# Attention beside two scans: TensorE's order written out in bursts, groups and scan parts

## The chip, the core and the metric

The kernel runs on one core of a Trainium2 chip. The metric is the device time of one execution in microseconds (us). TensorE (PE in the rows) multiplies matrices, VectorE (DVE), ScalarE (ACT) and GpSimd (POOL) work on elements, and SyncE (SP) issues most transfers.

## The reference

One layer of a hybrid encoder on 2048 tokens of width 1024: one input projection feeds attention with 8 heads (96 wide, values 64 wide, no mask) and an RWKV-7 mixer with 8 heads that is scanned forward and backward; both are gated and merged, and a mixture of 32 experts follows.

```python
h  = RMSNorm(x)
z  = h @ w_in
o1 = MLA(z_mla)        # softmax(q k^T / sqrt(96)) v, 8 heads, no mask
o2 = BiRWKV7(z_rwkv)   # forward and backward scans
m  = sigmoid(z_g1) * (o1 @ w_br_mla) + sigmoid(z_g2) * (o2 @ w_br_rwkv)
x  = x + m @ w_out
x  = x + HierMoE(RMSNorm(x))
```

## The kernel before

There are three phases. The first projects, normalizes and prepares operands. The second, `phase2`, holds attention and the scans, and is the one that changes. The third merges and runs the experts.

**Attention.** 8 heads times 4 blocks of 512 queries make 32 blocks. A block goes over 16 tiles of 128 keys. For each tile, `scores` forms a 128x512 bank of scores in three matmuls of split operands (L684 to L686), ScalarE takes the exponential into a tile `e` (L689), and VectorE (`accv`, odd tiles) or GpSimd (`acc`, even tiles) adds it up for the column sums. `av` multiplies four `e` tiles at a time with the values (L703). `finish` closes a block: column sums by matmuls (L713), the reciprocal (L716), four transposes (L719) and the product (L721). The exponential needs the row maxima beforehand, so `smax` (L664, one matmul, reduced by VectorE at L665) runs 24 tiles ahead of the scores, and `mrow` (L668 to L672) folds a block's maxima into its query operand. Scores, maxima, sums and transposes share a ring of four PSUM banks, `s`.

**The scans.** 32 steps, each for both directions (d = 0, 1). `operands` prepares a step ahead of time: two groups of products (L960, the "products" of a direction), masked by VectorE (L962), "inner" (L968) with its mask (L969), and two groups of transposes ("tokens", L975) of tiles that GpSimd scaled (L952), copied by ScalarE (L976). `step` is a chain: "state" (L1000, and its part of the output at L1013), copied out as `rs` by VectorE for d = 0 (L1008) and ScalarE for d = 1 (L1006); "solve" (L1021), copied to `mv` by VectorE and ScalarE (L1023, L1024); "update" (L1049), added into the next `mv` by VectorE (L1052); and "output" (L1031), copied by ScalarE (L1035). Each of these groups has two halves, one a direction, of 8 matmuls, and both halves lie in one bank, `rec` or `sa`. The multiplies at L1003 decay the state.

**What sets the order.** The program is written as generators, and `phase2` starts scan steps by a rule of pace, 32 steps over 29 blocks. The scheduler then orders the instructions of each engine by its own simulation. On TensorE it interleaves matmuls of attention and scans freely. Only the four matmuls of `av` stand in an order written by hand.

Of the kernel before, what the change touches and what calls it, by code (L numbers as in the profile page):

```python
# [21 lines left out]
NT = T // 128  # L22
# [580 lines left out]
def attention(k, aside):  # L603
# [5 lines left out]
    with ExitStack() as ctx:  # L609
# [15 lines left out]
        def raw_tile(h):  # L625

            return p.tile([128, 512], F32, name="raw" if h else "e", bufs=2 if h else 7)[0:96]
# [48 lines left out]
        def scores(B, u):  # L676
            khi, klo = KT[B.h]
            B.e[u] = []
            for i in range(2):
                kb = 2 * u + i  # L680
                b, c = kb // 4, slice(kb % 4 * 128, kb % 4 * 128 + 128)
                next(first)
# [4 lines left out]
                e = p.tile([128, 512], F32, name="e", bufs=7)  # L687
# [8 lines left out]
        def av(B, us):  # L696

            order = [(u, i) for u in reversed(us) for i in (1, 0)]
            seen = [False, False]
            with tc.high_priority(), tc.manual_schedule(engines={nc.tensor.engine}):  # L700
                for u, i in order:
                    r = slice(i * 64, i * 64 + 64)
                    nc.tensor.matmul(B.o[r], VT[B.h][:, 2 * u + i], B.e[u][i], start=(us[0] == 0 and not seen[i]),  # L703
                                     stop=(us[-1] == NT // 2 - 1 and u == us[0]))
                    seen[i] = True
            for u in us:
                B.e.pop(u)

        def finish(B):
# [5 lines left out]
            rd = p.tile([128, 8], F32, name="rd")  # L715
            nc.vector.reciprocal(rd, t[:, 0:8])  # L716
            t = k.ps2.tile([128, 512], F32, name="s", bufs=4)
            for i in range(4):
                nc.tensor.transpose(t[0:64, i * 128:(i + 1) * 128], rd[:, 2 * i:2 * i + 1].to_broadcast([128, 64]),  # L719
                                    k.ident)  # L720
# [7 lines left out]
        BL = []  # L728

        def ahead():  # L730

            for h, qs in blocks:
                if qs == 0:
                    load_head(h)
                BL.append(load_q(h, qs))
                if qs == 0:
                    load_v(h)
                if len(BL) == 1:
                    yield
                for j in range(16):  # L740
                    smax(BL[-1], j)
                    yield
                mrow(BL[-1])
            while True:
                yield

        first = ahead()
        next(first)
        yield
        for _ in range(16):  # L750
            next(first)
        yield
        for _ in range(8):
            next(first)
        for n in range(len(blocks)):
            yield
            for u in range(8):
                if u == 0:
                    B = BL[n]
                    B.o = k.ps2.tile([128, 512], F32, name="o", bufs=1)  # L760
                    B.acc = p.tile([128, 512], F32, name="acc")
                    B.accv = p.tile([128, 512], F32, name="accv", bufs=1)
                    B.e = {}
                scores(B, u)
                if u in (2, 4, 6):
                    av(B, (u - 2, u - 1))
                if u == 4 and n:
                    finish(BL[n - 1])
                if u in (2, 6) and n > 4:
                    next(aside, None)  # L770
            nc.vector.tensor_tensor(B.acc, B.acc, B.accv, op=OP.add)
            av(B, (6, 7))
            B.ob = p.tile([64, 512], F32, name="ob", bufs=1)
            nc.scalar.copy(B.ob, B.o[64:128])
            nc.vector.tensor_tensor(B.ob, B.o[0:64], B.ob, op=OP.add)
        finish(BL[-1])


class Rwkv:
# [135 lines left out]
    def load(self, j):  # L915
# [5 lines left out]
        bk = p.tile([128, 2, 2, 4, 2, 64], F32, name="bk", bufs=1)  # L921
        mv = p.tile([128, 2, 2, 2, 4, 64], F32, name="mv")
        ys = p.tile([128, 2, 2, 4, 64], F32, name="ys", bufs=1)
        self.pair[j] = st, bk, mv, ys
# [15 lines left out]
    def operands(self, n):  # L940
        k, p = self.k, self.p
        nc = k.nc
        if n % 2 == 0:
            self.load(n // 2)
        st, bk, _, _ = self.pair[n // 2]
        bs = p.tile([128, 2, 4, 128], F32, name="bks", bufs=1)
        ar = p.tile([128, 2, 4, 64], F32, name="arb")
        bt = p.tile([128, 2, 8, 64], F32, name="bkt")
        self.ops[n] = ar, bt
        for d in range(2):  # L950
            c, s = self.where(n, d)
            nc.gpsimd.tensor_tensor(bs[:, d], bk[:, s, d].rearrange("p g b t -> p g (b t)"),  # L952
                                    k.wc[:, d, :, c:c + 1].to_broadcast([128, 4, 128]), op=OP.mult)
        for d in range(2):
            c, s = self.where(n, d)
            m = self.mask[:, d:d + 1].to_broadcast([128, 4, 128])
            tv = self.bank("sa").rearrange("p (g t) -> p g t", t=128)
            for g in range(4):
                for e, r, ro in self.HEADS:
                    nc.tensor.matmul(tv[ro, g], bk[r, s, d, g, 1 - e], st[r, s, e, d, g], start=True, stop=True)  # L960
            for e, r, ro in self.HEADS:
                nc.vector.tensor_tensor(st[ro, s, e, d].rearrange("p g a t -> p g (a t)"), tv[ro], m[ro], op=OP.mult)  # L962
# [8 lines left out]
        for e, r, _ in self.HEADS:  # L971
            tv = self.bank("sa").rearrange("p (q t) -> p q t", t=64)
            for q in range(8):
                d, g = divmod(q, 4)
                nc.tensor.transpose(tv[:, q], bs[r, d, g], k.ident[r, r])  # L975
            nc.scalar.copy(bt[:, e], tv)  # L976

    def step(self, n):
        k, p = self.k, self.p
        nc, S = k.nc, k.scratch  # L980
        rd, i = divmod(n, 4)
        st, _, mv, ys = self.pair[n // 2]
        ar, bt = self.ops.pop(n)
        tt = self.tt[rd]
        Q = (slice(0, 4), slice(4, 8))
        bank = lambda name: self.bank(name).rearrange("p (q f) -> p q f", f=64)
# [5 lines left out]
        m0 = p.tile([128, 8, 64], F32, name="m0", bufs=1)  # L992
        t = bank("rec")
        y = bank("yy")
        rs = p.tile([128, 8, 64], F32, name="rs", bufs=1)
# [20 lines left out]
        t = bank("rec")  # L1016
        for d in range(2):
            c, s = self.where(n, d)
            for g in range(4):
                for e, r, _ in self.HEADS:  # L1020
                    nc.tensor.matmul(t[r, 4 * d + g], tt[r, d, g, i if d == 0 else 3 - i], rs[r, 4 * d + g],  # L1021
# [4 lines left out]
        def output():  # L1026
            for d in range(2):
                c, s = self.where(n, d)
                for g in range(4):
                    for e, r, _ in self.HEADS:  # L1030
                        nc.tensor.matmul(y[r, 4 * d + g], ar[r, d, g], mv[r, s, e, d, g], start=False,  # L1031
                                         stop=(d == 1 and g == 3))
            for d in range(2):
                c, s = self.where(n, d)
                nc.scalar.copy(ys[:, d, s], y[:, Q[d]])  # L1035
                if n % 2:
                    c0 = n - 1 if d == 0 else 31 - n
                    for e, r, _ in self.HEADS:
                        nc.sync.dma_start(S["y"][d, c0 * 64:c0 * 64 + 128, e * 256:e * 256 + 256]
                                          .rearrange("(c t) x -> t c x", t=64),  # L1040
                                          ys[r, d].rearrange("p s g f -> p s (g f)"))

        if n < 31:
            t = bank("rec")
            for d in range(2):
# [5 lines left out]
                for e, r, _ in self.HEADS:  # L1051
                    nc.vector.tensor_tensor(mn[r, sn, e, d], t[r, Q[d]], m0[r, Q[d]], op=OP.add)  # L1052
        output()


def rwkv(k, R):
    R.steps()
    R.operands(0)
    R.load_tt(0)
    yield  # L1060
    for n in range(32):
# [815 lines left out]
```

## Time and profile before

| | us |
|---|---|
| median of 3 runs | 3668.69 (3665.12 to 3672.79) |
| the profiled execution | 3667.47 |
| its span | 3665.7 |
| TensorE busy (matmul) in the span | 3390.9 (93%) |
| VectorE | 2570.1 (70%) |
| ScalarE | 1496.8 (41%) |
| GpSimd | 1395.7 (38%) |

The span runs from the first to the last instruction of the profiled execution. An engine's busy time is the time in which at least one of its instructions was running. The shares are means over three phases with different limits; the rows further down take the second phase by itself.

### The profile page before, as it was taken

Reading aid. Unit: us, or ns where it says so; the run is one execution under the profiler, and the core shown is the slowest. Engines: PE = TensorE matmul, PEld = TensorE weight load, DVE = VectorE, ACT = ScalarE, POOL = GpSimd, SP = SyncE. Lnnn points to the kernel's source line nnn. Section 1 sums busy time; section 2 is a strip of 40 time slices with the busy share of each in tenths; the row PEclk is TensorE's granted clock in tenths of the full one; section 3 lists DMA queues with packets and bytes.
Section 4 is the critical chain, followed back from the end, with each engine's and each line's share of the span. In section 5 each row is a group of like instructions: output and inputs, shape, how many; then the busy total and the mean of one; then the engine's idle time right before and its main releaser. Section 6 shows DMA issues by size and latency. Waiting matters only on the chain. (4 is left out here: it accounts for less than half of the span.)

```text
span 3665.7 us, 66865 instructions
## 1 busy us (share of the span) xinstructions
PE 3390.9 (93%) x25104; PEld 2448.3 (67%) x25104; DVE 2570.1 (70%) x4799; ACT 1496.8 (41%) x2834; POOL 1395.7 (38%) x1301
## 2 busy tenths in 40 slices
PE   8999999999988889999999999999689997999991
PEld 6778777777766656666666666655477886666660
DVE  6845677777887766676666666667766776678777
ACT  5322444445343333333333333334322222677772
POOL 1022322334222344444444444434423232665554
PEclk9999999999998889999999999999799998999995
DMA  5545767676554352233233332210545444788987
GB/s 177 170 150 171 218 197 208 197 200 202 202 179 144 114 135 77 72 106 97 74 110 96 94 92 66 56 36 12 164 144 150 135 131 169 283 319 322 336 328 301
DMA packets 392837, 589.71 MB, mean 161 GB/s; under 512 B 66880, under 2 KB 245184, under 8 KB 392512
## 3 DMA queue, kind: packets, MB, share of 16 engines
q1 hardware_dynamic: 380016, 546.36, 47.0%
q0 software_dynamic: 11920, 38.30, 2.8%
q8 instruction: 199, 3.26, 0.4%
q14 instruction: 126, 1.03, 0.1%
q10 hardware_dynamic: 576, 0.76, 0.1%
HBM read 380.78 MB, written 204.51 MB: 160 GB/s over the span
## 5 line engine op out<-in xcount | busy, mean ns | idle before, releaser
L689 ACT ACTIVATE e<-s 128x512 f32<-128x512 f32 x512 | 305.1, 597 | 547.3 <-PE s L686 534.8
L665 DVE TENSOR_REDUCE mx<-s 128x1 f32<-128x512 f32 x512 | 345.6, 684 | 240.2 <-PE s L664 236.6
L145 PE MATMUL z<-hhi,wlo 128*128 128x512 f32 (+1 forms) x1184 | 470.0, 397 | 2.4 <-POOL wlo L136 2.4
L144 PE MATMUL z<-hlo,whi 128*128 128x512 f32 (+1 forms) x1184 | 470.9, 398 | 0.2 <-DVE hlo L188 0.2
L694 POOL TENSOR_TENSOR acc<-acc,e 128x512 f32<-128x512 f32 x224 | 291.7, 1302 | 470.1 <-ACT e L689 460.5
L143 PE MATMUL z<-hhi,whi 128*128 128x512 f32 (+1 forms) x1184 | 469.2, 397 | 0.7 <-ACT hhi L187 0.3
L136 POOL TENSOR_TENSOR wlo<-wraw,whi 128x1024 fp32r<-128x1024 f32 x61 | 151.7, 2488 | 310.8 <-ACT whi L135 263.8
L145 PEld LDWEIGHTS z<-hhi,wlo 128*128 128x128 f32 (+1 forms) x1184 | 222.4, 188 | 62.4 <-issue 8.8
L144 PEld LDWEIGHTS z<-hlo,whi 128*128 128x128 f32 (+1 forms) x1184 | 222.5, 188 | 56.5 <-issue 3.9
L143 PEld LDWEIGHTS z<-hhi,whi 128*128 128x128 f32 (+1 forms) x1184 | 222.4, 188 | 55.0 <-issue 3.0
L703 PE MATMUL o<-e,v 128*64 128x512 f32 x1024 | 247.9, 602 | 4.5 <-ACT e L689 4.5
L694 DVE TENSOR_TENSOR accv<-accv,e 128x512 f32<-128x512 f32 x224 | 200.9, 897 | 71.8 <-ACT e L689 70.3
L498 ACT CAST wh<-wr 128x1024 fp32r<-128x1024 f32 x198 | 204.3, 1047 | 107.4 <-PE y L1578 54.0
L684 PE MATMUL s<-qhi,kh 128*128 128x512 f32 x512 | 236.7, 462 | 0.1
L499 POOL TENSOR_TENSOR wl<-wr,wh 128x1024 fp32r<-128x1024 f32 x70 | 186.8, 2690 | 124.8 <-ACT wh L498 124.7
L664 PE MATMUL s<-kh,qhi 128*128 128x512 f32 x512 | 227.5, 451 | 7.2 <-ACT qhi L498 6.8
L499 DVE TENSOR_TENSOR wl<-wr,wh 128x1024 fp32r<-128x1024 f32 x128 | 185.5, 1455 | 63.7 <-ACT wh L498 58.8
L685 PE MATMUL s<-qlo,kh 128*128 128x512 f32 x512 | 203.7, 398 | 0.0
L686 PE MATMUL s<-qhi,kl 128*128 128x512 f32 x512 | 203.1, 397 | 0.0
L684 PEld LDWEIGHTS s<-qhi,kh 128*128 128x128 f32 x512 | 96.4, 188 | 90.8 <-issue 68.6
L664 PEld LDWEIGHTS s<-kh,qhi 128*128 128x128 f32 x512 | 98.3, 193 | 55.2 <-issue 21.2
L703 PEld LDWEIGHTS o<-e,v 128*64 128x64 f32 x1024 | 66.6, 136 | 92.4 <-issue 80.0
(485 smaller groups left out, 8112.5 us busy)
## 6 DMA issues: line engine op xcount, KB each, us to landing
wr<-w_exp SPq DMA_DIRECT2D x198, 512.0 KB
wraw<-w_in SPq DMA_DIRECT2D x61, 512.0 KB
s_ye<-ye SPq DMA_DIRECT2D x33, 512.0 KB
s_ar<-ar SPq DMA_DIRECT2D x64, 256.0 KB
s_bk<-bk SPq DMA_DIRECT2D x64, 256.0 KB
s_zg<-zo SPq DMA_DIRECT2D x64, 256.0 KB
bk<-s_bk SPq DMA_DIRECT2D x32, 512.0 KB
stk<-s_ar SPq DMA_DIRECT2D x64, 256.0 KB
```

Source lines behind the costliest of these rows:

```text
L143: nc.tensor.matmul(t[:rows], hi[:, c, :rows], hhi[b][:, c], start=(c == 0), stop=False)
L144: nc.tensor.matmul(t[:rows], hi[:, c, :rows], hlo[b][:, c], start=False, stop=False)
L145: nc.tensor.matmul(t[:rows], lo[:, c, :rows], hhi[b][:, c], start=False, stop=(c == 7))
L498: k.nc.scalar.copy(hi, src)
L499: (eng or k.nc.vector).tensor_tensor(lo, src, hi.bitcast(F32), op=OP.subtract)
L664: nc.tensor.matmul(t, B.qhi[:, i * 128:(i + 1) * 128], KT[B.h][0][b], start=True, stop=True)
L665: nc.vector.tensor_reduce(B.mx[:, i, b:b + 1], t, axis=AX.X, op=OP.max)
L684: nc.tensor.matmul(t, khi[b][:, c], B.qhi, start=True, stop=False)
L685: nc.tensor.matmul(t, khi[b][:, c], B.qlo, start=False, stop=False)
L689: nc.scalar.activation(e, t, AF.Exp, scale=scale)
L694: eng.tensor_tensor(a, a, e, op=OP.add)
L703: nc.tensor.matmul(B.o[r], VT[B.h][:, 2 * u + i], B.e[u][i], start=(us[0] == 0 and not seen[i]), stop=(us[-1] == NT // 2 - 1 and u == us[0]))
```

## The change

TensorE's instructions of phase 2 are put under `manual_schedule`: they run as they are written, and the scheduler orders the other engines alone. The program is written anew for it.

A block is four quarters. A quarter is a burst of four times one maximum and one score (16 matmuls), then one part of a scan step, then the value products of the quarter before (4 matmuls), then another part. A step has seven parts: products of d = 0 and GpSimd's scaling; state; products of d = 1; solve and the first tokens; the other tokens; update and output; inner and the loads. Eight slots a block for seven parts give 8/7 step a block, so the scans end with block 28.

Beside that: the column sums stand a part ahead of the rest of `finish` (`sums`, `finish`), and the fold of `accv` into `acc` (`total`) and the output copies (`out`) follow a quarter later. `e` has 9 buffers (7 before), `accv` and `bk` two each (one before). The copy `rs` of d = 0 moves from VectorE to ScalarE. Loads of a scan pair are issued two pairs ahead. The first loads of attention are issued ahead of the scan's first operands. The counts of matmuls do not change.

```diff
-    def operands(self, n):
+    def products(self, n, d):
...
-            if d:
-                nc.scalar.copy(rs[:, Q[d]], t[:, Q[d]])
-            else:
-                nc.vector.tensor_copy(rs[:, Q[d]], t[:, Q[d]])
+            nc.scalar.copy(rs[:, Q[d]], t[:, Q[d]])
...
+        with tc.manual_schedule(engines={nc.tensor.engine}):
+            for n in range(len(blocks)):
+                B = BL[n]
+                B.acc = p.tile([128, 512], F32, name="acc")
+                B.accv = p.tile([128, 512], F32, name="accv")
+                B.e = {}
+                for v in range(4):
+                    scores(B, 2 * v)
+                    scores(B, 2 * v + 1)
+                    if v == 2 and n:
+                        sums(BL[n - 1])
+                    next(scan, None)
+                    if v:
+                        if v == 1:
+                            B.o = k.ps2.tile([128, 512], F32, name="o", bufs=1)
+                        av(B, (2 * v - 2, 2 * v - 1))
+                    elif n:
+                        av(BL[n - 1], (6, 7))
+                        out(BL[n - 1])
+                    next(scan, None)
+                    if v == 0 and n:
+                        total(BL[n - 1])
+                    if v == 2 and n:
+                        finish(BL[n - 1])
+                    if due:
+                        mrow(due.pop())
+                    if v % 2 and n > 4:
+                        next(aside, None)
...
+EB = 9
...
 def rwkv(k, R):
+
     R.steps()
-    R.operands(0)
+    R.load(0)
     R.load_tt(0)
+    for d in range(2):
+        R.products(0, d)
+    R.decayed(0)
+    for e in range(2):
+        R.tokens(0, e)
+    R.inner(0)
+    R.load(1)
     yield
     for n in range(32):
+        m = n + 1 if n < 31 else None
         if n % 4 == 0 and n < 28:
             R.load_tt(n // 4 + 1)
-        if n < 31:
-            R.operands(n + 1)
-        R.step(n)
+        if m:
+            R.products(m, 0)
+            R.decayed(m)
         yield
+        R.state(n)
+        yield
+        if m:
+            R.products(m, 1)
+        yield
+        R.solve(n)
+        if m:
+            R.tokens(m, 0)
+        yield
+        if m:
+            R.tokens(m, 1)
+        yield
+        R.update(n)
+        yield
+        if m:
+            R.inner(m)
+        if n % 2 and n // 2 + 2 < 16:
+            R.load(n // 2 + 2)
+        yield
+    R.ctx.close()
```

How the order moves is seen in three places in the middle of the stage. First TensorE around a solve, before; each row is a line, an operation, and what it writes and reads.

```order
L664 MATMUL s<-kh_12737,qhi_13324 128x512
L684 MATMUL s<-qhi_12773,kh_14127 128x512
L685 MATMUL s<-qlo_12774,kh_14127 128x512
L686 MATMUL s<-qhi_12773,kl_14129 128x512
L975 MATMUL sa<-cst,bks 128x64 x3
L703 MATMUL o<-e,v 64x512 x4
L664 MATMUL s<-kh_12746,qhi_13324 128x512
L1021 MATMUL rec<-rs,tt 64x64 x8
L684 MATMUL s<-qhi_12773,kh_14127 128x512
L685 MATMUL s<-qlo_12774,kh_14127 128x512
L686 MATMUL s<-qhi_12773,kl_14129 128x512
```

The eight matmuls at L1021 are one half of solve; score matmuls of attention stand on both sides, and the other half follows seven rows on. The same place of the changed kernel, with the semaphores that an instruction waits on; its lines are L716 for the sums, L968 for products, L701 for value products, L1053 for solve and L990 for tokens.

```order
L664 MATMUL s<-kh_13918,qhi_13080 128x512 [waits DVE_49]
L684 MATMUL s<-qhi_12679,kh_13909 128x512 [waits Activation_49]
L685 MATMUL s<-qlo_12680,kh_13909 128x512
L686 MATMUL s<-qhi_12679,kl_13911 128x512
L716 MATMUL s<-cst,acc 128x2 [waits DVE_49]
L716 MATMUL s<-cst,acc 128x2 x3
L968 MATMUL sa<-stk,bk 64x128 x8
L701 MATMUL o<-e,v 64x512 x4
L1053 MATMUL rec<-rs,tt 64x64 x8
L1053 MATMUL rec<-rs,tt 64x64 [waits Activation_49]
L1053 MATMUL rec<-rs,tt 64x64 x7
L990 MATMUL sa<-cst,bks 128x64 [waits PE_49,Pool_49]
```

The two halves of solve now stand back to back, and the first matmul of the second half waits on ScalarE. Next TensorE around an update, before.

```order
L1049 MATMUL rec<-mv,bkt 64x64 x3
L684 MATMUL s<-qhi_12773,kh_14127 128x512
L685 MATMUL s<-qlo_12774,kh_14127 128x512
L686 MATMUL s<-qhi_12773,kl_14129 128x512
L1049 MATMUL rec<-mv,bkt 64x64 x2
L664 MATMUL s<-kh_12737,qhi_13324 128x512
L1049 MATMUL rec<-mv,bkt 64x64 x3
```

One half of update stands in three pieces between score matmuls. The update of the changed kernel (L1069, output L1078), behind a group of value products:

```order
L990 MATMUL sa<-cst,bks 128x64 x8
L701 MATMUL o<-e,v 64x512 x4
L1069 MATMUL rec<-mv,bkt 64x64 x8
L1069 MATMUL rec<-mv,bkt 64x64 [waits DVE_49]
L1069 MATMUL rec<-mv,bkt 64x64 x7
L1078 MATMUL yy<-mv,arb 64x64 x16
```

Both halves and the output stand in one piece, the second half with a wait on VectorE. Last VectorE around an update, before.

```order
L721 TENSOR_TENSOR ob<-s,ob 64x512
L665 TENSOR_REDUCE mx<-s 128x1 x2
L1052 TENSOR_TENSOR mv<-rec,m_23721 64x256 x2
L665 TENSOR_REDUCE mx<-s 128x1
L694 TENSOR_TENSOR accv<-accv,e 128x512
L962 TENSOR_TENSOR stk<-sa,mask 64x512 x2
L665 TENSOR_REDUCE mx<-s 128x1
L1052 TENSOR_TENSOR mv<-rec,m_23721 64x256 x2
L1003 TENSOR_TENSOR m_24126<-mv,wc 64x256 x2
L665 TENSOR_REDUCE mx<-s 128x1
```

The two adds of a half (L1052) come with reductions of maxima between the halves. VectorE of the changed kernel, with L1072 for the adds, L710 for the fold of `accv`, L1034 for the decay and L1004 for inner's mask:

```order
L665 TENSOR_REDUCE mx<-s 128x1 x3
L694 TENSOR_TENSOR accv<-accv,e 128x512
L665 TENSOR_REDUCE mx<-s 128x1
L1072 TENSOR_TENSOR mv<-rec,m_18501 64x256
L694 TENSOR_TENSOR accv<-accv,e 128x512
L1072 TENSOR_TENSOR mv<-rec,m_18501 64x256
L710 TENSOR_TENSOR acc<-acc,accv 128x512
L1072 TENSOR_TENSOR mv<-rec,m_18501 64x256 x2
L1034 TENSOR_TENSOR m_18865<-mv,wc 64x256 x2
L1004 TENSOR_TENSOR arb<-sa,mask 128x256 x2
L665 TENSOR_REDUCE mx<-s 128x1 x3
```

A burst's reductions now come together, an add into `accv` stands between the two adds of update's first half, and the fold of `accv` ahead of those of the second.

## Rows read from the trace of the kernel before

**Rows 1.** Windows of all engines; after busy times the granted clock, DMA's share, GB/s.
```profile
1297.65:1420.00 122.35, 113.24 (x1226) 78.90 (x1226) 80.50 (x136) 40.81 (x76) 48.99 (x50) 0.93 0.46 120
1420.00:2400.00 980.00, 978.32 (x9008) 614.46 (x9003) 666.27 (x1096) 346.76 (x650) 437.13 (x417) 1.00 0.30 84
2400.00:2587.20 187.20, 174.67 (x925) 105.63 (x923) 125.98 (x187) 75.72 (x133) 84.35 (x68) 0.99 0.09 24
```
**Rows 2.** Timeline of TensorE around an update: start, duration, line, operation, count.
```profile
1701.97 0.50 PE L684 MATMUL s<-qhi,kh 128*128 128x512 f32 x1
...
1703.10 0.56 PE L1049 MATMUL rec<-mv,bkt 128*64 128x64 f32 x10
```
**Rows 3.** Timeline of TensorE in two late blocks, without scans.
```profile
2505.22 0.51 PE L684 MATMUL s<-qhi,kh 128*128 128x512 f32 x1
...
2509.10 1.94 PE L703 MATMUL o<-e,v 128*64 128x512 f32 x8
2510.97 0.51 PE L684 MATMUL s<-qhi,kh 128*128 128x512 f32 x1
...
2520.20 1.94 PE L703 MATMUL o<-e,v 128*64 128x512 f32 x8 [0.69 <-ACT e L689]
...
2524.36 0.95 PE L713 MATMUL s<-cst,acc 128*128 128x2 f32 x8
2526.51 1.02 PE L719 MATMUL s<-cst,rd 128*64 128x128 f32 x4 [1.21 <-DVE rd L716]
```
**Rows 4.** Timeline of all engines around the first solve.
```profile
1323.64 0.63 PE L1021 MATMUL rec<-rs,tt 64*64 64x64 f32 x16
...
1324.32 0.42 DVE L1023 COPY mv<-rec 64x256 f32<-64x256 f32 x1
...
1324.82 0.37 ACT L1024 COPY mv<-rec 64x256 f32<-64x256 f32 x1 [1.69 <-DVE mv L1023]
...
1325.24 0.68 PE L1021 MATMUL rec<-rs,tt 64*64 64x64 f32 x16
...
1325.76 0.63 PE L1031 MATMUL yy<-mv,arb 64*64 64x64 f32 x14
```
**Rows 5.** Timeline of TensorE: output and products of a step, then tokens.
```profile
1464.62 0.69 PE L1013 MATMUL yy<-mv,stk 128*64 128x64 f32 x16
1465.24 1.09 PE L960 MATMUL sa<-stk,bk 64*64 64x128 f32 x16
1466.26 0.57 PE L1000 MATMUL rec<-mv,stk 128*64 128x64 f32 x12
...
1724.93 0.71 PE L975 MATMUL sa<-cst,bks 64*128 64x64 f32 x8
1725.56 0.68 PE L1021 MATMUL rec<-rs,tt 64*64 64x64 f32 x16
```
**Rows 6.** Lines of VectorE from 1420 to 2400: busy us, mean ns, idle before.
```profile
L665 DVE TENSOR_REDUCE mx<-s 128x1 f32<-128x512 f32 x368 | 249.9, 685 | 186.2 <-PE s L664 183.8
L694 DVE TENSOR_TENSOR accv<-accv,e 128x512 f32<-128x512 f32 x161 | 143.2, 889 | 50.4 <-ACT e L689 49.6
L962 DVE TENSOR_TENSOR stk<-sa,mask 64x512 f32<-64x512 f32 x108 | 74.3, 688 | 13.0 <-PE sa L960 11.0
L1052 DVE TENSOR_TENSOR mv<-rec,m 64x256 f32<-64x256 f32 x108 | 45.2, 418 | 12.9 <-PE rec L1049 11.5
L1003 DVE TENSOR_TENSOR m<-mv,wc 64x256 f32<-64x256 f32 x54 | 36.8, 718 | 0.5
...
L969 DVE TENSOR_TENSOR arb<-sa,mask 128x256 f32<-128x256 f32 x56 | 23.3, 416 | 4.8 <-PE sa L968 4.2
```
**Rows 7.** Timeline of TensorE at the stage's start.
```profile
1323.12 0.68 PE L968 MATMUL sa<-stk,bk 64*64 64x64 f32 x16
...
1333.79 0.80 PE L664 MATMUL s<-kh,qhi 128*128 128x512 f32 x1 [6.76 <-ACT qhi L498]
```
**Rows 8.** Window of TensorE around the wait at 2526: busy, clock, DMA, GB/s.
```profile
2520.00:2530.00 10.00, 8.59 (x37) 0.83 0.00 0
```

More of the change, by code (lines that the diff above doesn't have):

```diff
@@ L600, in up_kv, with attention @@
             yield
-def attention(k, aside):
+def attention(k, scan, aside):
     nc, tc, S = k.nc, k.tc, k.scratch
@@ L696, in av, with out, total, sums @@
         def av(B, us):
[L698 to L701, printed above, removed]
+            for u in us:
+                for i in range(2):
                     r = slice(i * 64, i * 64 + 64)
[L703 to L706, printed above, removed]
+                    nc.tensor.matmul(B.o[r], VT[B.h][:, 2 * u + i], B.e[u][i], start=(u == 0), stop=(u == NT // 2 - 1))
                 B.e.pop(u)
-        def finish(B):
+        def out(B):
+            B.ob = p.tile([64, 512], F32, name="ob", bufs=1)
+            nc.scalar.copy(B.ob, B.o[64:128])
+            nc.vector.tensor_tensor(B.ob, B.o[0:64], B.ob, op=OP.add)
+        def total(B):
+            nc.vector.tensor_tensor(B.acc, B.acc, B.accv, op=OP.add)
+        def sums(B):
             t = k.ps2.tile([128, 512], F32, name="s", bufs=4)
@@ L747, in attention @@
-        first = ahead()
-        next(first)
-        yield
[L750 to L771, printed above, removed]
-            av(B, (6, 7))
-            B.ob = p.tile([64, 512], F32, name="ob", bufs=1)
-            nc.scalar.copy(B.ob, B.o[64:128])
-            nc.vector.tensor_tensor(B.ob, B.o[0:64], B.ob, op=OP.add)
@@ L776, in attention, with ahead @@
-        finish(BL[-1])
+        BL, at, due = [], [0], []
+        def ahead(n):
+            for _ in range(n):
+                m, j = divmod(at[0], 16)
+                at[0] += 1
+                if m == len(blocks):
+                    at[0] -= 1
+                    return
+                if j == 0:
+                    h, qs = blocks[m]
+                    if qs == 0:
+                        load_head(h)
+                    BL.append(load_q(h, qs))
+                    if qs == 0:
+                        load_v(h)
+                smax(BL[m], j)
+                if j == 15:
+                    due.append(BL[m])
@@ new lines, in attention @@
+        ahead(16)
+        mrow(due.pop())
+        yield
+        ahead(8)
+        with tc.manual_schedule(engines={nc.tensor.engine}):
[23 more added lines that the diff above has]
+                    if due:
+                        mrow(due.pop())
+                    if v % 2 and n > 4:
+                        next(aside, None)
+            av(B, (6, 7))
+            total(B)
+            out(B)
+            sums(B)
+            finish(B)
@@ L938, in where @@
         return (n, n % 2) if d == 0 else (31 - n, 1 - n % 2)
-    def operands(self, n):
[L941 to L949, printed above, removed]
+    def products(self, n, d):
+        st, bk, _ = self.pair[n // 2]
+        nc = self.k.nc
+        c, s = self.where(n, d)
+        m = self.mask[:, d:d + 1].to_broadcast([128, 4, 128])
+        tv = self.bank("sa").rearrange("p (g t) -> p g t", t=128)
+        for g in range(4):
+            for e, r, ro in self.HEADS:
+                nc.tensor.matmul(tv[ro, g], bk[r, s, d, g, 1 - e], st[r, s, e, d, g], start=True, stop=True)
+        for e, r, ro in self.HEADS:
+            nc.vector.tensor_tensor(st[ro, s, e, d].rearrange("p g a t -> p g (a t)"), tv[ro], m[ro], op=OP.mult)
@@ L950, in operands, with decayed @@
+    def decayed(self, n):
+        k = self.k
+        bk = self.pair[n // 2][1]
+        self.bs = self.p.tile([128, 2, 4, 128], F32, name="bks", bufs=1)
+        self.ops[n] = [None, self.p.tile([128, 2, 8, 64], F32, name="bkt")]
         for d in range(2):
             c, s = self.where(n, d)
[L952 to L962, printed above, removed]
+            k.nc.gpsimd.tensor_tensor(self.bs[:, d], bk[:, s, d].rearrange("p g b t -> p g (b t)"),
+                                      k.wc[:, d, :, c:c + 1].to_broadcast([128, 4, 128]), op=OP.mult)
@@ new lines, in tokens, with inner @@
+    def tokens(self, n, e):
+        k = self.k
+        r = self.HEADS[e][1]
+        tv = self.bank("sa").rearrange("p (q t) -> p q t", t=64)
+        for q in range(8):
+            d, g = divmod(q, 4)
+            k.nc.tensor.transpose(tv[:, q], self.bs[r, d, g], k.ident[r, r])
+        k.nc.scalar.copy(self.ops[n][1][:, e], tv)
+    def inner(self, n):
+        nc = self.k.nc
+        st, bk, _ = self.pair[n // 2]
+        ar = self.ops[n][0] = self.p.tile([128, 2, 4, 64], F32, name="arb")
@@ L970, in operands, with wide, state @@
                                     self.mask[:, d:d + 1, 64:128].to_broadcast([128, 4, 64]), op=OP.mult)
[L971 to L978, printed above, removed]
-        k, p = self.k, self.p
[L980 to L986, printed above, removed]
+    Q = (slice(0, 4), slice(4, 8))
+    def wide(self, name):
+        return self.bank(name).rearrange("p (q f) -> p q f", f=64)
+    def state(self, n):
+        k, p = self.k, self.p
+        nc, Q = k.nc, self.Q
+        st, _, mv = self.pair[n // 2]
         if n == 0:
@@ L1014, in step, with solve @@
                                      start=(d == 0 and g == 0), stop=False)
-        t = bank("rec")
+    def solve(self, n):
+        nc, Q = self.k.nc, self.Q
+        mv, tt = self.pair[n // 2][2], self.tt[n // 4]
+        i = n % 4
+        t = self.wide("rec")
         for d in range(2):
@@ L1024, in step, with update @@
             nc.scalar.copy(mv[self.O, s, 1, d], t[self.O, Q[d]])
[L1026 to L1041, printed above, removed]
+    def update(self, n):
+        nc, S, Q = self.k.nc, self.k.scratch, self.Q
+        mv = self.pair[n // 2][2]
+        ar, bt = self.ops.pop(n)
         if n < 31:
-            t = bank("rec")
+            t = self.wide("rec")
             for d in range(2):
@@ L1091, in phase2 @@
         scans = rwkv(k, k.R)
+        att = attention(k, scans, clear(k, pc))
+        next(att)
         next(scans)
[L1094 to L1108 removed]
         for _ in att:
```

80 lines of the change are left out of this document (34 added, 46 removed).

## The prediction

> **What bounds the kernel now.** The stage that changes is attention with the scans, and I read the windows of all engines over it first. It runs from the end of the first block's maxima at 1297.65 to the last matmul at 2587.2, 1289.5 us of the span of 3665.7. Between 1420 and 2400, where the scans run beside attention, TensorE is busy 978.3 of 980.0 us at a granted clock of 1.00, VectorE 666 and the other two less than half [rows 1]. So TensorE alone sets the pace there, and nothing waits. 23 blocks and 27 scan steps fit in these 980 us: 42.6 us a block at 1.17 steps, or about 42.2 at 8/7 steps, the change's pace (0.03 steps less, at the 10 to 13 us that a step comes to below).
>
> TensorE's time there is not all columns. Second view, its timeline. Four score matmuls that stand alone, between the two pieces of an update, take 1703.10 - 1701.97 = 1.13 us [rows 2]. In the late blocks, where no scan is left, sixteen in a row take 2509.10 - 2505.22 = 3.88, that is 0.23 each plus 0.20 once [rows 3]. Each change of kind thus costs 0.15 to 0.20 us. In the order of before the score matmuls stand in 547 runs, in that of after in 131.
>
> **The change, part by part.** *What a block costs when TensorE waits for nothing.* Attention: four bursts of sixteen, 4 x 3.88; four groups of products, 4 x (2510.97 - 2509.10) = 4 x 1.87; the column sums, 2526.51 - 1.21 - 2524.36 = 0.94, and some 0.65 for the two small groups like them [rows 3]. That is 24.6. A scan step: 1.02 for each of two products (1465.24 to 1466.26) and 0.63 for each of two token transposes; of the six other groups of two halves each (state, its output part, solve, update, output, inner) eight halves at 0.52 and four, the first of their slot, at 0.62 (1464.62 to 1465.24) [rows 4, 5]. Sum 2.04 + 1.26 + 4.16 + 2.48 = 9.94, and 11.4 at 8/7 steps. A block would take 36.0 us, 6.2 below the 42.2 of before. That is the gain on offer, and it comes wholly from fewer changes of kind.
>
> *What the written order adds: waits inside a part.* The second half of state, solve, update and inner writes the bank from which the first half's readers still read, and the order shows a wait in front of it, in after as in before. In before other matmuls stood between the halves; now nothing does. The price can be read at the start of the stage, where nothing was left to put between: solve's first half starts at 1323.64 and needs 0.52, VectorE copies at 1324.32 (0.42), ScalarE at 1324.82 (0.37), and the second half starts at 1325.24, not 1324.16: 1.08 us [rows 4]. The hand-overs in it are 0.16 from TensorE to a reader and 0.05 back. Update waits for two adds, 2 x 0.42 + 0.21 and the gap between them, 1.1; inner for one mask, 0.42 + 0.21 = 0.63 to 0.67; state for ScalarE's one copy, 0.37 + 0.21, say 0.62 [rows 4, 6]. Together 3.47 a step, 3.97 a block. These waits need no queue: they are there with every reader idle.
>
> *Waits behind VectorE's queue.* The written order puts a part right behind a burst half of the time. VectorE then still has the burst's last reductions and the add into accv (0.89) ahead of the part's adds [rows 6]; the order shows it between two of update's adds. About 1.5 x 8/7 parts a block with a VectorE wait stand there; with half an add each, 0.75 a block. The bounds are 0 (VectorE through in time) and 1.5 (a whole add each).
>
> The other side is the burst's start. Its third maximum takes the bank of the first, and can't start until that one is reduced: 4 x 0.23 x 2 = 1.84 us after the burst's start. VectorE may be held by the part before: two masks of 0.69 after products, two adds of 0.42 and two multiplies of 0.72 after update [rows 6]. With masks ending 1.58 after the burst's start, the first reduction ends 2.27, which costs TensorE 0.5. I take 0.5 for each of the four bursts, 2.0 a block; bounds 0 (in the late blocks bursts with nothing before them run without a wait, [rows 3]) and 3.0.
>
> The block's sum is then 36.0 + 3.97 + 0.75 + 2.0 = 42.7, against 42.2: the waits (6.7) eat the gain.
>
> *Late blocks.* The scans end with block 28 of 32; four remain, each 24.6 plus the wait for the exponential before the products, 0.69 [rows 3], 25.3. The wait of 1.21 for the reciprocal [rows 3] goes, since the sums now stand a part ahead of the transposes. No maxima remain for the last 24 key tiles: -24 x 0.23 = -5.5.
>
> *Start.* The scan's first operands now stand ahead of block 0's scores in TensorE's order, and are loaded no earlier. In before they end at about 1323.6 [rows 7], with block 0's scores around them and 6.76 us of waiting for a query block behind them. After starts block 0 at 1323.6, with that wait gone, since the query comes in meanwhile. Bounds: block 0 starts at 1320, or the 6.76 stays.
>
> *Sum.* 1323.6 + 28 x 42.7 + 4 x 25.3 - 5.5 = 2614.9.
>
> *Clock.* Where TensorE was held for 1.21 us the mean granted clock of 10 us was 0.83 [rows 8], with matmuls at the 1.2 GHz level behind the wait; the whole late stretch, 7% idle, has 0.99, the full stretch 1.00 [rows 1]. At 16% idle (6.7 of 42.7) I take 0.98: 36 x 0.02 = 0.7 a block, half of it swallowed by waits that shrink, 0.36 x 28 = 10 us. Bounds 0 and the rival below. The Trainium skill, "TensorE: Matmul & The Clock Gate", section "A second HAM failure mode: psum-queue depth-cycling", describes a kernel whose short idles between groups of matmuls made the clock swing between its levels. By that rule the clock is the larger loss; the late rows, at 0.99 with a wait a block, bear it out only weakly.
>
> 2614.9 + 10 - 2587.2 = 37.7 (some 14 from the 28 blocks, 10 from the clock, the rest from the start) over the profiled execution's 3667.5, so 3705.2; the median of the runs shown is 1.2 above that execution, and I keep **3705 us**.
>
> *Edits at nothing.* Two more e buffers, a second accv and bk: no instruction changes, and the reuse waits that they lift were hidden in a full stretch. The first rs copy moves from VectorE to ScalarE (347 of 980 us busy), 32 x 0.4; it is inside the 0.62 of state. Loads of a pair are issued two pairs ahead, over 70 us, with DMA at 0.30 [rows 1]; if that cover failed, products would wait.
>
> **Rivals.** *VectorE is in time* (chance 0.25). Only the waits inside parts remain, 4.0 a block: 28 x 2.7 = 76 us less and some 4 of clock, **3625**, faster. For it: VectorE is at 68%, and reductions in the late bursts keep up. Against: the written order gives it work in lumps. It decides by the waits of a block: 5.4 us give no change ((3705 - 3669) / 28 = 1.3 below 6.7), under 5.2 the kernel is faster by more than 0.2% (7.3 us), which is about what a measurement of this kernel can tell from none.
>
> *The halves do not wait* (0.04). If a second half could start while the first half's columns are read, 4.7 a block go: 3705 - 132 - 7 = **3566**. The order shows the wait on 32 of 32 steps, so this needs readers that finish before TensorE asks. The Trainium skill, "PSUM — Partial Sum Buffer", section "PSUM bank collisions raise a hardware error", says that the compiler's scheduler makes any two engines that touch one bank and quadrant wait for each other, other columns or not. The 1.08 us in the rows agrees with that.
>
> *The clock swings* (0.11). At a mean of 0.94 (the first stretch, with its waits, had 0.93 [rows 1]) the matmuls of a block take 36 x 0.06 = 2.2 longer, 61 us in place of 10: **3756**.
>
> *No change* (0.10): waits between 5.2 and 5.7 a block.
>
> The forecast, slower by over 0.2%, has 0.50, and the clock rival is slower too: slower 0.61, same 0.10, faster 0.29. The range goes down to 3615, a little below the first rival (its start at 1320 and full clock), and up to 3760: all bounds of the queue waits together, 8.5 a block, give 3755, the clock rival 3756. It leaves out the rival without waits and the tails, under 2 in 10.
>
> **What would show it.** In the profile of after, between two blocks with scans: TensorE idle 6 to 7 us of 43, most of it ahead of the second halves, released by ScalarE in solve and state and VectorE in update and inner, about 1.1, 0.6, 1.1 and 0.65 each; waits of about 0.5 at a burst's third maximum, released by reductions; bursts of 3.9. A granted clock from 0.97 to 0.99 there. Block 0's scores behind the scan's operands, at 1323. The forecast is wrong if a step's waits inside parts are well under 3.5 us, if bursts wait for nothing, or if the clock leaves that band.

## The result and the profile after

The changed kernel takes 3732.59 us (median of 4 runs, 3723.98 to 3735.61) against 3668.78 (4 runs): a ratio of 1.017, 95% interval 1.0149 to 1.0191. It is slower, as forecast, by 64 us where 36 were forecast, and inside the range. The profiled execution took 3723.98 us, 8.6 below the median, with a span of 3722.2. The last matmul of the stage ends at 2642.1; the forecast had 2624.9, before had 2587.2.

The windows of all engines, as in [rows 1]:

```profile
1297.65:1420.00 122.35, 101.40 (x999) 71.29 (x1000) 72.29 (x118) 40.73 (x75) 46.29 (x46) 0.85 0.42 108
1420.00:2400.00 980.00, 848.11 (x8550) 582.15 (x8549) 653.83 (x1025) 342.92 (x649) 426.80 (x404) 0.97 0.30 84
```

TensorE, full before, now stands idle 980 - 848.1 = 131.9 us between 1420 and 2400, and the granted clock is 0.97. No other engine has become the bound: VectorE is at 67%. Where the idle time lies is read from the lines of TensorE in the same stretch; the last columns are the idle time ahead of a line and what ended it (L1053 solve, L1069 update, L1003 inner, L1030 state).

```profile
L701 PE MATMUL o<-e,v 128*64 128x512 f32 x712 | 179.7, 627 | 0.0
L664 PE MATMUL s<-kh,qhi 128*128 128x512 f32 x356 | 154.7, 434 | 1.0 <-DVE mx L665 1.0
L684 PE MATMUL s<-qhi,kh 128*128 128x512 f32 x356 | 148.7, 418 | 17.0 <-ACT e L689 15.7 <-DVE qhi L672 0.5
...
L1053 PE MATMUL rec<-rs,tt 64*64 64x64 f32 x800 | 36.0, 233 | 38.0 <-ACT mv L1056 38.0
L1003 PE MATMUL sa<-stk,bk 64*64 64x64 f32 x832 | 35.4, 224 | 22.7 <-DVE arb L1004 22.7
L1069 PE MATMUL rec<-mv,bkt 128*64 128x64 f32 x832 | 35.3, 228 | 39.1 <-DVE mv L1072 39.1
L1030 PE MATMUL rec<-mv,stk 128*64 128x64 f32 x800 | 34.0, 228 | 14.1 <-ACT rs L1031 14.1
```

356 maxima are 22.25 blocks; 800 to 832 records of 32 a step are 25 to 26 steps. Of the 131.9 us, 113.9 stand ahead of the four second halves: 1.52 us for each solve, 1.50 update, 0.87 inner, 0.56 state. The bursts have 18.0, 0.81 a block.

How one of these waits comes about, in the timeline of all engines around a solve (answers to [rows 4]):

```profile
1796.81 1.30 POOL L694 TENSOR_TENSOR acc<-acc,e 128x512 f32<-128x512 f32 x1
1796.84 1.82 DVE L694 TENSOR_TENSOR accv<-accv,e 128x512 f32<-128x512 f32 x1
...
1800.63 1.39 DVE L970 TENSOR_TENSOR stk<-sa,mask 64x512 f32<-64x512 f32 x2
1800.74 0.68 PE L1053 MATMUL rec<-rs,tt 64*64 64x64 f32 x16
...
1801.94 0.67 DVE L710 TENSOR_TENSOR acc<-acc,accv 128x512 f32<-128x512 f32 x1
1802.54 0.41 DVE L1055 COPY mv<-rec 64x256 f32<-64x256 f32 x1
1803.04 0.37 ACT L1056 COPY mv<-rec 64x256 f32<-64x256 f32 x1 [3.92 <-DVE mv L1055]
1803.46 0.68 PE L1053 MATMUL rec<-rs,tt 64*64 64x64 f32 x16 [2.03 <-ACT mv L1056]
```

VectorE still has the masks of the products two slots earlier and the fold of accv when solve's first half is done; its copy starts at 1802.54, and TensorE stands idle 2.03 us. Counted as [rows 4] were, from the end of the first half's issue, that is 2.20 us in place of 1.08. Around an update it is `out` that stands ahead:

```profile
1812.56 0.64 PE L1069 MATMUL rec<-mv,bkt 128*64 128x64 f32 x16
...
1813.44 0.68 DVE L707 TENSOR_TENSOR ob<-o,ob 64x512 f32<-64x512 f32 x1 [1.46 <-ACT ob L706]
...
1814.05 0.85 DVE L1072 TENSOR_TENSOR mv<-rec,m 64x256 f32<-64x256 f32 x2
...
1814.95 0.69 PE L1069 MATMUL rec<-mv,bkt 128*64 128x64 f32 x16 [1.75 <-DVE mv L1072]
```

Behind the wait of 2.03 us the score matmuls stand 0.43 us apart in place of 0.23. Window from 1803.4, granted clock next to last but two:

```profile
1803.40:1808.20 4.80, 4.74 (x33) 3.86 (x34) 1.80 (x3) 1.55 (x4) 0.61 (x1) 0.66 0.12 30
```

It is 0.66 there, mostly the 1.2 GHz level. So this wait cost its own time and then more in the burst behind it.

The start, timeline of TensorE (answers to [rows 7]):

```profile
1306.56 0.50 PE L684 MATMUL s<-qhi,kh 128*128 128x512 f32 x1
...
1313.65 0.65 PE L968 MATMUL sa<-stk,bk 64*64 64x128 f32 x2 [3.06 <-issue]
1315.38 1.96 PE L968 MATMUL sa<-stk,bk 64*64 64x128 f32 x14 [1.08 <-DMA stk<-s_ar]
1318.94 0.66 PE L968 MATMUL sa<-stk,bk 64*64 64x128 f32 x2 [1.59 <-DMA stk<-s_ar]
...
1324.21 1.08 PE L990 MATMUL sa<-cst,bks 64*128 64x64 f32 x8 [1.57 <-DVE stk L970]
...
1329.52 1.12 PE L1003 MATMUL sa<-stk,bk 64*64 64x64 f32 x16 [0.53 <-DVE arb L1004]
...
1337.38 0.50 PE L664 MATMUL s<-kh,qhi 128*128 128x512 f32 x1
```

Block 0's first burst runs from 1306.56, ahead of the scan's first operands, which come behind it, wait for their loads and end at 1330.6 (1329.52 + 1.12). Products take 1.96 in place of 1.02 there, the lower clock again: the granted clock is 0.50, the 1.2 GHz level, from 1313.6 to 1331. Block 0's second burst starts at 1337.4, behind one burst, the operands, one group of products and one state.

### The profile page after: what moved, and what is told of

Read it like the earlier page. It is cut to its first block, busy times and chain, and to the rows that moved or that the text cites. A ratio compares the mean times of both kernels' runs of the same rounds, so it can differ in the third digit from the quotient of the medians.

```text
span 3722.2 us, 66958 instructions
## 1 busy us (share of the span) xinstructions
PE 3297.7 (89%) x25104; PEld 2447.8 (66%) x25104; DVE 2590.2 (70%) x4767; ACT 1508.5 (41%) x2866; POOL 1399.6 (38%) x1301
## 5 line engine op out<-in xcount | busy, mean ns | idle before, releaser
L694 DVE TENSOR_TENSOR accv<-accv,e 128x512 f32<-128x512 f32 x224 | 242.3, 1082 | 41.0 <-ACT e L689 39.3
L701 PE MATMUL o<-e,v 128*64 128x512 f32 x1024 | 256.4, 623 | 0.0
L684 PE MATMUL s<-qhi,kh 128*128 128x512 f32 x512 | 212.4, 415 | 19.8 <-ACT e L689 16.7
L970 DVE TENSOR_TENSOR stk<-sa,mask 64x512 f32<-64x512 f32 x128 | 88.2, 689 | 77.0 <-PE sa L968 75.0
```

The costliest lines, as they stand in the source:

```text
L684: nc.tensor.matmul(t, khi[b][:, c], B.qhi, start=True, stop=False)
L694: eng.tensor_tensor(a, a, e, op=OP.add)
```

## The experiments

The ratio in each is to the kernel before, run on the same chip.

**e1. Halves apart.** `state`, `solve`, `update` and `inner` become generators that yield behind their first half, and `rwkv` puts the two halves of each into neighbouring slots; still seven slots a step.

```diff
...
+        v = R.solve(n)
+        next(v)
         if m:
             R.products(m, 0)
             R.decayed(m)
         yield
-        R.state(n)
-        yield
+        next(v)
         if m:
             R.products(m, 1)
         yield
...
```

> The two halves of state, solve, update and inner are put into neighbouring slots, so that a burst or a group of value products stands between them; everything else stays as in the changed kernel (seven slots a step, the same matmuls). Theory (waits inside parts): TensorE's idle time ahead of second halves in the changed kernel is 114 us between 1420 and 2400 for some 25.5 steps, 4.5 us a step, 142 us over 32 steps; 1.87 us of products or a burst of 3.9 us covers nearly all of it, and the clock comes back with it: 142 less 15 that stay, and 20 to 30 us of clock, so 3575 to 3595. Rival (VectorE's lumps set the pace, and the wait only moves to the next burst): idle time of the stage stays over 4 us a block, 3660 to 3700. Rival (clock not tied to these waits): 3605 with a granted clock still at 0.97.

3553.75 us, ratio 0.9685 (0.9669 to 0.9701): 179 us below the changed kernel and 115 below the kernel before. That is 21 us under the theory's range, and far from both rivals. Window and lines of TensorE, 1420 to 2400 (L1056 solve, L1073 update, L1031 state):

```profile
1420.00:2400.00 980.00, 941.25 (x9760) 649.27 (x9756) 758.76 (x1185) 398.29 (x754) 486.55 (x455) 0.98 0.32 90
```
```profile
L664 PE MATMUL s<-kh,qhi 128*128 128x512 f32 x420 | 180.9, 431 | 15.8 <-ACT e L689 11.1 <-DVE mx L665 4.3
L684 PE MATMUL s<-qhi,kh 128*128 128x512 f32 x420 | 171.7, 409 | 18.1 <-ACT e L689 14.4 <-DVE mx L665 3.3
...
L1056 PE MATMUL rec<-rs,tt 64*64 64x64 f32 x928 | 40.8, 229 | 0.0
...
L1003 PE MATMUL sa<-stk,bk 64*64 64x64 f32 x912 | 39.1, 225 | 0.0
L1031 PE MATMUL rec<-mv,stk 128*64 128x64 f32 x928 | 39.0, 226 | 0.0
L1073 PE MATMUL rec<-mv,bkt 128*64 128x64 f32 x896 | 37.2, 226 | 0.0
```

The waits ahead of second halves are gone: idle time falls from 131.9 to 38.7, with VectorE up to 77%. A small part of them moved: the bursts wait 15.8 + 18.1 = 33.9 us, 1.29 a block in place of 0.81. 941.25 us for 26.25 blocks are 35.9 us of TensorE's work a block, with 28 to 29 steps in the records, some 1.1 a block; the prediction's 36.0 at 8/7 holds within 2%.

**e2. Only solve and update apart.**

> Only solve and update are split over two slots; state and inner keep their halves together, and products and tokens move to make room. Theory: the waits of solve and update, 77 of the 114 us of idle time between 1420 and 2400, 3.0 us a step, 97 us in all, go, less some 5 that stay, with 15 of clock: 3625. If state's and inner's short waits (0.5 to 0.9 us) cost clock as well, the gain of this run is less than two thirds of the gain of the run that splits all four. Rival (VectorE's lumps): 3690.

3596.13 us, ratio 0.9796 (0.9779 to 0.9813), 29 us under the theory's 3625. State and inner keep their waits:

```profile
1420.00:2400.00 980.00, 908.87 (x9540) 630.28 (x9539) 718.80 (x1134) 380.47 (x721) 467.54 (x439) 0.99 0.31 87
```
```profile
L1003 PE MATMUL sa<-stk,bk 64*64 64x64 f32 x928 | 39.8, 225 | 25.8 <-DVE arb L1004 25.8
...
L1030 PE MATMUL rec<-mv,stk 128*64 128x64 f32 x928 | 39.7, 229 | 20.9 <-ACT rs L1031 20.9
```

Of e1's gain of 179 us this run has 136, 76%, though solve and update held 77 of 114 us of idle time, 68%. The granted clock is 0.99 between 1420 and 2400, not 0.97, with inner waiting 25.8 / 29 = 0.89 us each step and state 0.72. So nearly all that the clock lost went with the waits of solve and update, the longer ones.

**e3. TensorE's order left to the scheduler.** The changed program, `if True:` in place of `manual_schedule`.

> The changed program as it is, but TensorE's order left to the scheduler again (no manual_schedule). Theory (the written order is what costs, all else is at nothing): 3669, within 10 us of the kernel before, TensorE idle under 1% between 1420 and 2400. Rival (the rest of the change, program order, late sums, the copy moved to ScalarE, costs too): 3690 to 3715.

3781.94 us, ratio 1.031 (1.0293 to 1.0327): both expectations were too low. TensorE is full and does less: 344 scores, 21.5 blocks, where the kernel before did 23.

```profile
1420.00:2400.00 980.00, 979.26 (x8308) 585.31 (x8310) 609.08 (x993) 328.38 (x627) 402.71 (x388) 1.00 0.29 81
```

**e5. The same, with `av` as in the kernel before**: its four matmuls together, at high priority.

> As the run with the scheduler, but the four matmuls of a group of value products keep together, as in the kernel before. Theory now (TensorE full all the time, so that changes of kind are all that differ): the order has 1834 changes of kind in the stage against 1741 of the kernel before, 1904 of the free scheduler and 663 of the changed kernel; 93 more than before at 0.17 to 0.2 us are 16 to 19 us, so 3685. Rival (a single value product between score matmuls is dear by itself, over 0.2 us each): with the groups whole, nearly all of the 113 us that the free scheduler lost comes back, 3670 or under. Rival (the rest of the change costs): stays above 3720.

3699.72 us, ratio 1.0074 (1.0057 to 1.0091): above the theory's 3685, and none of the rivals. With the value products together, 86 of e3's 113 us are gone (112.8 and 27.1 us over the kernel before, each on its own chip): in e3 they stand in 284 runs in the order, here in 127. What remains is 27 us over the kernel before, for 93 more changes of kind, 0.29 us each, more than the 0.20 that [rows 3] give. So "all else at nothing" fails for the scheduler's own order; which part of the program makes it worse was not tried. Against the same program under the scheduler, the changed kernel's order is 49 us faster than e3's and 33 slower than this one; only with the halves apart, in e1, is the order by hand well ahead of all of them, 146 us below this run.

**e4. Start spread.** The scan's first operands as four parts in block 0's slots. (In the changed kernel they stand behind block 0's first burst, as the start's rows show, and not ahead of its scores.)

> The scan's first operands are taken as four parts of their own in block 0's slots, instead of standing ahead of block 0's scores; the loads stay where they are. Theory: at the start TensorE is idle 11 us in all between 1310 and 1335 and runs its 12 us of matmuls there at the lower clock; with attention's bursts beside them 12 to 16 us are saved: 3716. Rival (the scans' data come so late that the same waits stand in block 0's slots): 3726 to 3732, no change.

3719.52 us, ratio 1.0147 (1.0129 to 1.0166), 13 us below the changed kernel; the intervals overlap, so this size is not settled. The profile shows a new wait, 8.40 us at 1341.94, for a query block's cast.

**e6. e1 with the start spread.**

> The run with halves in neighbouring slots, with the scan's first operands taken in six slots of block 0 as well. Theory (the two gains lie in different places and add): 12 us below the run with halves, 3541. Rival (with the halves apart the start is covered in part already): 3548 to 3554.

3554.97 us, ratio 0.9678 (0.9662 to 0.9694): no change from e1; the rival holds. The gain at the start is given back a little later, timeline of TensorE:

```profile
1341.06 0.80 PE L664 MATMUL s<-kh,qhi 128*128 128x512 f32 x1 [10.79 <-ACT qhi L498]
```

**e7. Filler in the waits.** The changed kernel with useless work between the halves of solve and update; its output is unchanged.

```diff
+    def fill(self):
+        t = self.k.ps2.tile([128, 512], F32, name="s", bufs=4)
+        for _ in range(4):
+            self.k.nc.tensor.matmul(t, *self.filler, start=True, stop=True)
...
+            if d == 0:
+                self.fill()
...
+                if d == 0:
+                    self.fill()
```

> The changed kernel with four more score-like matmuls (128x512, 0.92 us, into a score bank that nothing reads) between the two halves of solve and of update: TensorE does useless work in waits of 1.5 us. Theory (the low clock comes from these waits): the clock between 1420 and 2400 rises from 0.97 to 0.99 and the kernel gets 15 to 35 us faster, though it does 63 x 0.92 = 58 us more work: 3697 to 3717. Rival (the waits cost only their own time, clock the same): 3730 to 3740, as the filler stays inside the waits. Rival (the filler waits for a score bank and delays the second half): 3745 to 3780.

3711.22 us, ratio 1.010 (1.0083 to 1.0117): 21 us faster than the changed kernel with 58 us more work.

```profile
1420.00:2400.00 980.00, 902.81 (x8883) 615.84 (x8883) 661.57 (x1038) 348.47 (x658) 431.65 (x409) 0.98 0.31 85
```
```profile
L1047 PE MATMUL s<-kh,qhi 128*128 128x512 f32 x204 | 62.0, 426 | 0.0
...
L1059 PE MATMUL rec<-rs,tt 64*64 64x64 f32 x800 | 35.4, 230 | 12.2 <-ACT mv L1062 12.1
L1077 PE MATMUL rec<-mv,bkt 128*64 128x64 f32 x832 | 35.0, 226 | 12.7 <-DVE mv L1080 12.3
```

The filler (L1047) takes the place of idle time, 25 us left of 77, and the clock rises by 0.01. 361 maxima, 22.56 blocks, fit in the stretch. Idle time and filler together are (77.2 + 62.0) / 22.56 = 6.2 us a block, where idle time alone was 5.9: the waits did not get shorter. All other matmuls take (902.8 - 62.0) / 22.56 = 37.3 us a block in place of 38.1, and 0.85 x 28 blocks are 24 us. So the gain lies in matmuls that run faster: the part of the loss that is clock is thereby shown, not only read off.

**e8. Half bursts.** e1 with the first slot of a quarter in the middle of the burst.

```diff
                     scores(B, 2 * v)
-                    scores(B, 2 * v + 1)
                     if v == 2 and n:
                         sums(BL[n - 1])
                     next(scan, None)
+                    scores(B, 2 * v + 1)
```

> The run with halves, but the first slot of a quarter stands in the middle of the burst: two runs of 8 score matmuls in place of one of 16, 116 more changes of kind in the stage (913 against 797). Theory (changes cost 0.17 to 0.2 us each): 20 to 23 us more work; the waits at bursts, 34 us between 1420 and 2400, shrink by half, 17 x 1.3 = 22 us less: no change, 3545 to 3560. Rival (VectorE's queue behind bursts is the last limit): waits vanish, 3525. Rival (waits stay and the changes come on top): 3575.

3544.22 us, ratio 0.9651 (0.9635 to 0.9667), 0.3% below e1. Between theory and first rival: idle time falls from 38.7 to 21.2, the clock goes from 0.98 to 1.00, and that is worth more than the 116 changes of kind.

```profile
1420.00:2400.00 980.00, 958.82 (x9822) 648.48 (x9818) 773.72 (x1202) 405.66 (x766) 493.07 (x461) 1.00 0.33 90
```

**e9. e8 with the start spread and the second pair's loads later.**

> The run with half bursts, with the scan's first operands in six slots of block 0 and the loads of the second scan pair issued behind the first operands. Theory: in the run that only spread the first operands, TensorE later stood 10.8 us for a query block's cast, whose load waited behind the second pair's; with that load first the 11 us come back, 3533 against 3544 without. Rival (the first pair's own loads are what the query block waits for): the wait stays, 3541 to 3547.

3544.84 us, ratio 0.9667 (0.9651 to 0.9684): no change from e8, inside the rival's range. TensorE waits 12.51 us for the cast, and SyncE's own timeline shows why:

```profile
1329.15 1.68 SPq L854 DMA_DIRECT2D tt<-s_tt  x2
1330.88 0.50 SPq L655 DMA_DIRECT2D e<-s_qt  x1
```

The edit had not moved the query's load (L655): it was still issued behind all of the scan's, so that this run does not tell which of them it waits for.

**e11. e9 with query blocks 1 and 2 loaded beside block 0's.**

```diff
-                    BL.append(load_q(h, qs))
+                    if m not in (1, 2):
+                        BL.append(load_q(h, qs))
+                    if m == 0:
+                        BL.extend(load_q(0, i) for i in (1, 2))
```

> As the run with half bursts and spread first operands, but the query blocks 1 and 2 are loaded together with block 0's, ahead of every scan load in the program and in SyncE's order. In the run before, the load of query block 2 was issued at 1330.9, behind the scan's loads, and TensorE stood 12.5 us for its cast. Theory: that wait goes and nothing takes its place, 3531 to 3534 against 3544. Rival (another late load, block 3's query or the second pair, makes TensorE wait as long a little later): 3541 to 3546.

3531.89 us (5 runs), ratio 0.9635 (0.9622 to 0.9648), as expected, and the fastest of all: 3.65% under the kernel before. The first stretch now has a clock of 0.93 and no wait for a query:

```profile
1297.65:1420.00 122.35, 113.12 (x1112) 76.82 (x1112) 90.36 (x141) 47.38 (x88) 55.00 (x55) 0.93 0.41 107
```

**e10. The copy rs of the first direction back on VectorE**, in the changed kernel.

> The changed kernel with the copy rs of the first direction back on VectorE, as before the change. Theory (a wait inside a part is as long as its reader's queue): state's second half, which waited 0.55 us a step for ScalarE, waits for VectorE like update's, 0.9 to 1.5 us, so 11 to 30 us slower than the changed kernel: 3743 to 3762. Rival (the copy is at nothing on either engine): 3728 to 3737.

3736.12 us, ratio 1.0187 (1.0168 to 1.0205), not to be told from the changed kernel's 1.017. Lines of TensorE (L1056 solve, L1072 update, L1003 inner, L1030 state):

```profile
L1056 PE MATMUL rec<-rs,tt 64*64 64x64 f32 x800 | 36.2, 233 | 34.6 <-ACT mv L1059 34.6
L1072 PE MATMUL rec<-mv,bkt 128*64 128x64 f32 x816 | 34.6, 228 | 37.5 <-DVE mv L1075 37.5
L1003 PE MATMUL sa<-stk,bk 64*64 64x64 f32 x800 | 34.5, 226 | 19.9 <-DVE arb L1004 19.9
L1030 PE MATMUL rec<-mv,stk 128*64 128x64 f32 x800 | 34.1, 228 | 21.5 <-DVE rs L1034 21.5
```

State waits longer, 0.86 us a step in place of 0.56, and the other three a little less; the four together have 113.5 us, where the changed kernel had 113.9. The theory falls: the copy is at nothing.

## Why the prediction was right, and where its terms were off

**The gain on offer**, 36.0 us a block without waits: right (e1, e8).

**Waits inside parts**: right in place and cause. Every second half was released by the engine that was named, and e1 took the whole loss away by putting other work between the halves. The Trainium skill, "PSUM — Partial Sum Buffer", section "PSUM bank collisions raise a hardware error", says that the compiler's scheduler puts a dependency between any two engines that touch one bank and quadrant. The traces agree: no second half starts ahead of its bank's reader, at 1.08 us [rows 4] or 2.03.

**Waits behind VectorE's queue**: the step that was mis-sized, in both directions. Ahead of the halves 0.75 a block was allowed for half an add into accv; masks, the fold of accv and `out`'s add stand there too, and an add into accv took 1.09 us in this stretch, not 0.89 (the last section has the reason). Idle time of 4.45 us a step, with 0.16 for each half's drain (a half shows 0.68 where its matmuls are issued in 0.52), makes 5.1 against 3.47 + 0.66 = 4.1 predicted: 1.0 x 32 = 31 us more. At the bursts 2.0 a block were allowed and 0.81 measured, 33 us less. And the releaser was another: scores wait for the exponential of the bank's last user (15.7 of 18 us), the third maximum hardly for its reduction (1.0). The two errors cancel, which is luck; a block's waits between 1420 and 2400 are 131.9 / 22.25 = 5.9 us, 6.6 with the drain, predicted 6.7.

**Clock**: 0.97, not 0.98. A block's TensorE time is 848.1 / 22.25 = 38.1; less 0.7 of drain, and less the 36.0 of work, 1.4 are left, against the 0.36 allowed. The granted clock is at the lower end of the band that was given, 0.97 to 0.99. Halving the clock's cost for "waits that shrink" was wrong: the waits are set by other engines' queues and the slow matmuls come behind them. The Trainium skill, "TensorE: Matmul & The Clock Gate", section "A second HAM failure mode: psum-queue depth-cycling", describes a kernel whose frequent short idles between groups of matmuls made the clock swing. e7 agrees: with filler in the idles the clock rose to 0.98 and 21 us came back, more than the 10 allowed for all of it.

**Start**: the order was read wrongly here. Block 0's scores were to stand behind the scan's operands; its first burst ran ahead of them, at 1306.56, and the operands are what the second burst waited for. 1323.6 as the operands' end in before was a misreading too: their tokens end at 1327.0.

```profile
1326.32 0.71 PE L975 MATMUL sa<-cst,bks 64*128 64x64 f32 x8
```

In after they end at 1330.6. Block 0 had a burst, products and a state behind it at 1337.4, 3.88 + 1.02 + 2.28 = 7.2 us of work, so it began as if at 1330.2, 6.6 later than forecast. The misreading alone is 3.4. Beside it, the first phase ended 4.3 us later (1301.4 for the fold of the first maxima against 1297.1) and the operands ran at the lower clock; what each of the three adds was not told apart. That the wait for a query goes was right only while the start was slow: in e4, e6 and e9 it was back.

**Late blocks**: from the end of the 28th block, 2545.7, to 2642.1 are 96.4 us; forecast 95.7. Right.

**The sum.** Between 1420 and 2400 a block takes 980 / 22.25 = 44.0 us against 43.1 with clock in the forecast, and the clock is what is more. The other 5.75 blocks with scans, the first and the last ones, took 41.0 on average, so that all 28, from 1330.2 to 2545.7, average 43.4, 10 us more than forecast. With 6.6 of start and 0.7 of late blocks that is the 17.2 us by which the stage ends later (2642.1 - 2624.9). The other 10 of the 27.6 us between 3705 and 3732.6 are 1.6 us behind the stage, and the profiled execution's place 8.6 below the median, for which the forecast added nothing.

**Rivals.** VectorE in time and halves that don't wait: ruled out by the lines. The clock's swing is there in part, at 0.97 and not 0.94.

## What to carry to other kernels

An order written by hand saves the changes of kind that a scheduler scatters, but it has to leave work between the two uses of one bank: look for every matmul whose bank was just handed to a reader, and put a group there that needs none of its readers. A wait of 2 us on TensorE cost more than 2 us here, since matmuls behind it ran at the lower clock (0.66 over 4.8 us). Matmuls that run side by side, like the two of a value pair below, have to stay together in the order. A stall that is removed at a stage's start often shows the next late load, so look at the queue's own order, not only at the code's.

## What was not expected

VectorE's add into accv took 889 ns in before [rows 6], and 1.82 us in the rows above, where GpSimd's add into acc ran beside it (1796.8); over the whole kernel its mean went from 897 to 1082 ns. In bursts these two adds often run together. The Trainium skill, "SBUF — State Buffer", section "Who interferes with whom", states that a VectorE instruction with two inputs in SBUF contends with a GpSimd instruction that reads SBUF, and calls the port pair that they share an exclusive lock. The trace of after agrees, when the 224 adds into accv are sorted by what GpSimd did meanwhile. The 23 with no tensor operation of GpSimd beside them took 673 to 694 ns; the 201 with one took 1128 ns on average, and 22 that start within 0.1 us of GpSimd's add into acc took 1844. In before 112 stood alone, at 686 ns, and 112 did not, at 1107. So it is not the add that got slower: more of them met GpSimd. No run here changed that alone.

Value products that stand singly between score matmuls are dear. From e3 to e5 157 runs of them and 86 us go, 0.55 us each, against 0.15 to 0.2 for a change of kind elsewhere; e5 also gave them high priority. e3's own timeline of TensorE has the reason, where a value product is two records:

```profile
2406.45 1.08 PE L701 MATMUL o<-e,v 128*64 128x512 f32 x4
2407.46 0.50 PE L684 MATMUL s<-qhi,kh 128*128 128x512 f32 x1
...
2408.35 1.07 PE L701 MATMUL o<-e,v 128*64 128x512 f32 x2
2409.36 0.51 PE L664 MATMUL s<-kh,qhi 128*128 128x512 f32 x1
```

Two products hold TensorE for 1.01 us to the next matmul, and one for 1.01 us as well. The two of a pair write different halves of `o` and run side by side (in the first group the records of one start 6 ns behind those of the other), so a product that is parted from its pair costs as much as the pair; a group of four takes 1.87 [rows 3].
